# Alternating seven-product groups with usual ones, new bank places and a second bias-line buffer in an encoder kernel

## Chip, cores and metric

The kernel runs on one core of a Trainium2 chip. The metric is the device time of one execution in microseconds (us). Three runs of the kernel before gave 2324.68, 2325.39 and 2327.51 us, median 2325.39.

## The reference

A trunk of two layers over 256 positions of width 2048, all in float32. Layer 0 mixes tokens by grouped-query attention (mixer A), layer 1 by dilated window attention in three head groups with a shared relative bias (mixer B). Each is followed by a gated MLP of inner width 5632 with a convolution of width 3:

```python
def conv_ffn(h, w_up, conv_w, conv_b, w_down):
    u = h @ w_up
    c = u.shape[-1]
    pad = CONV_WIDTH // 2
    u = lax.conv_general_dilated(u, conv_w[:, None, :].astype(u.dtype), window_strides=(1,),
                                 padding=((pad, pad),), dimension_numbers=('NWC', 'WIO', 'NWC'),
                                 feature_group_count=c) + conv_b
    gate, val = jnp.split(u, 2, axis=-1)
    return (jax.nn.silu(gate) * val) @ w_down
...
        h = h + conv_ffn(rms_norm(h, ffn_norm[i]), w_up[i], conv_w[i], conv_b[i], w_down[i])
    return rms_norm(h, final_norm)
```

In mixer B the bias of a head is a table looked up by the distance of query and key; the kernel builds each head's line of values once and writes it to DRAM.

## The kernel before

**Products of float32 in three.** TensorE multiplies a reduced float format, so each operand is split into a high and a low part, and a product is taken as high x high, high x low and low x high. Weights come in tiles of 128x1024 (512 KB) by SyncE's queue (load_raw, L127; feed_T, L134) into six raw buffers; ScalarE makes the high part wh (split_raw, L119), VectorE the low part wl (L120). The parts go into a ring of three pairs of tiles, and of a fourth from the FFN's own pool (hl_ring, L608) during the down projection.

**The FFN** runs in two halves of 6 and 5 chunks of 512 inner columns (HALVES, L21). In a half, the up projection (feed_T: L143 for wh, L146 for wl) fills two banks ga and two banks va for each half chunk; up_post adds the two results (v, L446), scales (L448), convolves (L450 to L457) and applies silu; glu multiplies and splits into the tiles of activations ah and al (L468), or glu_forms into the seven combinations that a seven-product group needs. Then the down projection of this half's chunks: column blocks n = 0 and 1 together in project_pair, in the first half also 2 and 3; in the second half n = 2 and 3 come one by one by project (L164 to L166). add_residual (L386) or done (L559) adds the result to h.

**project_pair** treats a chunk either as a *usual* group: four units of 12 matmuls (128x512), which add straight into the four result banks C11, C21 (units 0, 1; block n0) and C12, C22 (units 2, 3; block n1), or as a *seven-product* group after Strassen and Winograd: seven units of 6 matmuls. Products 2, 3 and 4 go into C11, C12 and C21, the products 1, 5, 6 and 7 into banks of their own (M1, M5, M6, M7) that combine (L613 to L627: one copy on ScalarE and eight operations of 128x512 on VectorE) adds into h once the last product of the pair is out. Products 5, 7, 6 and 4 need the sum of two raw tiles (prepare, L240, on VectorE, put ahead in the order by high_priority). In both halves chunks 0 and 2 are seven-product groups (SKG). MIX sets the order: each seven-product group is interleaved with one usual group, in places two products next to each other; the usual groups that remain follow.

**Banks.** [...] new_acc (L187) alternates between b0, b1 and b2, b3; b4 to b7 are also turned over for small work by ps_tile. project_pair takes b4 to b7 for M1, M5, M6, M7 and b0 to b3, always in this order, for C11, C21, C12, C22 (L217). Which pair the up projection has just filled, and which the next new_acc takes, is in bank_at[0] and doesn't enter.

**Order.** A scheduler sets each engine's order at build time from the program's order and priorities; split_raw and the sums are 45 places ahead (AHEAD). Work that follows a stage (up_post, combine, the bias lines) is held as generators, of which step() runs one piece after each unit.

**Bias lines.** bias_lines (L870 to L891) is the side work of layer 0's first up projection: for each of six lines a matmul into a small bank (L885), a copy by VectorE into a tile ln (L888) and four DMAs by SyncE's queue to DRAM (scr0, scr1, L891). The tile has the tag "junk", of which there is one buffer. Lines 1 and 2 are 512 wide, the other four 256; each is written as four pieces, one per 32 of the 128 rows.

## Time and profile before

| | |
|---|---|
| three runs, median | 2325.39 us |
| the profiled execution | 2326.31 us |
| its span | 2324.5 us |
| mean granted TensorE clock | 0.996 |
| TensorE matmuls, busy | 11569, 2290.6 us (99% of the span) |
| VectorE busy | 1751.6 us (75%) |
| ScalarE busy | 1256.6 us (54%) |
| GpSimd busy | 168.8 us (7%) |
| weight loads of w_up, w_down (512 KB), issue to landing | 5.0 us, 5.3 us |

PE is TensorE, DVE VectorE, ACT ScalarE, POOL GpSimd, SP SyncE with its DMA queue (SPq). A row "L120 DVE ... wl<-raw,wh" is line 120 of the kernel, on VectorE, from tiles raw and wh to wl. A row of the timeline gives start, duration, and at its end in brackets the engine's idle time ahead and what ended it. A duration of a matmul is longer than its distance to the next, since they overlap; distances are taken from start to start. The clock is the share of full speed that the chip granted TensorE.

### The profile page before, as it was taken

How to read it: one execution, taken by the hardware profiler on the slowest of the kernel's cores; microseconds unless marked ns; L12 is line 12 of the kernel's file. 1: busy time of each engine (PE TensorE's matmuls, PEld its weight loads, DVE VectorE, ACT ScalarE, POOL GpSimd, SP SyncE). 2: the span in 40 equal slices, each digit the busy share in tenths (PEclk: the TensorE clock that was granted, in tenths of full speed). 3: DMA queues.
4: the chain of work that ended last, by engine and by line, in shares of the span. 5: the costliest groups of instructions: out<-in, count | busy, mean ns of one | idle time of the engine just before them, and what ended most of it. 6: DMA issues, size and time to landing. Idle time of an engine off the chain costs nothing.

```text
span 2324.5 us, 31224 instructions
## 1 busy us (share of the span) xinstructions
PE 2290.6 (99%) x11569; PEld 1935.9 (83%) x11569; DVE 1751.6 (75%) x2513; ACT 1256.6 (54%) x1816; POOL 168.8 (7%) x130
## 2 busy tenths in 40 slices
PE   9999999999999999999999999999999999999998
PEld 7788788888888888788888888878888878888876
DVE  6877876778867778968776876586777787777784
ACT  6565564555546556555554554355555544565553
POOL 2210010010000110000000000000101000001110
PEclk9999999999999999999999999999999999999999
DMA  8445665665666565566655565566566566666663
GB/s 296 155 138 161 191 193 174 211 198 181 207 198 187 188 189 172 200 213 197 197 173 174 180 190 164 178 188 196 185 195 188 168 209 208 182 190 186 195 208 127
DMA packets 260313, 437.54 MB, mean 188 GB/s; under 512 B 13904, under 2 KB 196944, under 8 KB 260160
## 3 DMA queue, kind: packets, MB, share of 16 engines
q1 hardware_dynamic: 258080, 429.84, 58.7%
q0 software_dynamic: 1648, 5.15, 0.8%
q8 instruction: 90, 1.47, 0.3%
q14 instruction: 63, 0.52, 0.1%
q10 hardware_dynamic: 432, 0.56, 0.1%
HBM read 429.20 MB, written 6.29 MB: 187 GB/s over the span
## 4 chain that ended last, share of the span: by engine, by line
PE 89%; DVE 5%; DMA 1%; issue 1%; ACT 1%; POOL 1%; SPq 0%; POOLq 0%; DVEq 0%; ACTq 0%
PE acc L143 27%; PE acc L146 14%; PE acc L165 11%; PE acc L166 11%; PE acc L164 11%; PE acc L271 4%; PE acc L273 4%; PE acc L276 4%; DVE wl L120 2%; DVE tT L332 1%; ACT wh L119 1%; DMA scr<-ln 1%; PE ps L303 1%; POOL cv L465 1%; PE ps L307 1%
## 5 line engine op out<-in xcount | busy, mean ns | idle before, releaser
L119 ACT ACTIVATE wh<-raw 128x1024 fp32r<-128x1024 f32 x828 | 872.7, 1058 | 779.3 <-PE acc L166 284.3
L120 DVE TENSOR_TENSOR wl<-raw,wh 128x1024 fp32r<-128x1024 f32 x828 | 1014.1, 1230 | 363.5 <-ACT wh L119 349.9
L143 PE MATMUL acc<-xh,wh 128*128 128x512 f32 x2816 | 709.6, 394 | 0.8 <-DVE h L386 0.8
L143 PEld LDWEIGHTS acc<-xh,wh 128*128 128x128 f32 x2816 | 508.3, 189 | 93.8 <-ACT wh L119 2.1
L146 PEld LDWEIGHTS acc<-xh,wl 128*128 128x128 f32 x2816 | 385.8, 191 | 36.1 <-DVE wl L120 8.4
L146 PE MATMUL acc<-xh,wl 128*128 128x256 f32 x2816 | 394.9, 283 | 7.6 <-DVE wl L120 7.6
L165 PE MATMUL acc<-wl,xh 128*128 128x512 f32 x768 | 300.3, 391 | 3.9 <-DVE wl L120 2.4
L164 PE MATMUL acc<-wh,xh 128*128 128x512 f32 x768 | 301.8, 394 | 0.0
L166 PE MATMUL acc<-wh,xh 128*128 128x512 f32 x768 | 299.6, 390 | 0.0
L271 PE MATMUL acc<-wh,ah 128*128 128x512 f32 x520 | 204.7, 394 | 3.6 <-DVE v L446 3.6
L273 PE MATMUL acc<-wh,al 128*128 128x512 f32 x520 | 204.3, 393 | 0.0
L164 PE MATMUL acc<-wh,ah 128*128 128x512 f32 x480 | 188.8, 393 | 2.4 <-DVE h L386 2.0
L165 PE MATMUL acc<-wl,ah 128*128 128x512 f32 x480 | 189.2, 394 | 2.0 <-DVE wl L120 1.8
L166 PE MATMUL acc<-wh,al 128*128 128x512 f32 x480 | 187.8, 392 | 0.0
L165 PEld LDWEIGHTS acc<-wl,xh 128*128 128x128 f32 x768 | 144.4, 188 | 34.2 <-DVE wl L120 4.9
L166 PEld LDWEIGHTS acc<-wh,xh 128*128 128x128 f32 x768 | 144.2, 188 | 30.0
L164 PEld LDWEIGHTS acc<-wh,xh 128*128 128x128 f32 x768 | 144.4, 188 | 28.1
L276 PE MATMUL acc<-wl,ah 128*128 128x512 f32 x520 | 148.0, 393 | 2.5 <-DVE wl L120 2.5
L271 PEld LDWEIGHTS acc<-wh,ah 128*128 128x128 f32 x520 | 97.6, 188 | 27.2 <-DVE v L446 5.4
L276 PEld LDWEIGHTS acc<-wl,ah 128*128 128x128 f32 x520 | 97.0, 188 | 27.1 <-DVE wl L120 5.9
L273 PEld LDWEIGHTS acc<-wh,al 128*128 128x128 f32 x520 | 97.6, 188 | 21.8
L165 PEld LDWEIGHTS acc<-wl,ah 128*128 128x128 f32 x480 | 90.6, 189 | 24.2 <-DVE wl L120 5.8
(175 smaller groups left out, 1843.7 us busy)
## 6 DMA issues: line engine op xcount, KB each, us to landing
raw<-in_w_up_dram SPq DMA_DIRECT2D x352, 512.0 KB, 5.0
raw<-in_w_down_dram SPq DMA_DIRECT2D x176, 512.0 KB, 5.3
raw<-in_w_b_dram SPq DMA_DIRECT2D x144, 512.0 KB, 4.3
raw<-in_w_bo_dram SPq DMA_DIRECT2D x48, 512.0 KB, 3.6
raw<-in_w_a_dram SPq DMA_DIRECT2D x40, 512.0 KB, 4.1
raw<-in_w_ao_dram SPq DMA_DIRECT2D x32, 512.0 KB, 3.5
raw<-in_w_a_dram SPq DMA_DIRECT2D x16, 256.0 KB, 5.5
h<-in_x_dram SPq DMA_DIRECT2D x4, 512.0 KB
```

Source lines behind the costliest of these rows:

```text
L119: nc.scalar.activation(wh, r, AF.Copy)
L120: nc.vector.tensor_tensor(wl, r, wh.bitcast(F32), ALU.subtract)
L143: nc.tensor.matmul(acc[j], wh[:, kt, j * P:(j + 1) * P], lhs[4 * kg + kt][2], start=first and i == 0 and kt == 0, stop=False)
L146: nc.tensor.matmul(acc[j][:, :NT], wl[:, kt, j * P:(j + 1) * P], lhs[4 * kg + kt][0], start=False, stop=end and kt == 3)
L164: nc.tensor.matmul(accs[m], xh, wh[:, j, :], start=st, stop=False)
L165: nc.tensor.matmul(accs[m], xh, wl[:, j, :], start=False, stop=False)
L166: nc.tensor.matmul(accs[m], xl, wh[:, j, :], start=False, stop=sp)
L271: nc.tensor.matmul(acc[k], xh, wh[:, j, :], start=k in fresh, stop=False)
L273: nc.tensor.matmul(acc[k], xl, wh[:, j, :], start=False, stop=False)
L276: nc.tensor.matmul(acc[k], xh, wl[:, j, :], start=False, stop=last[k] == i and j == 1)
L303: nc.tensor.matmul(o, lh[ls], rh[rs], start=start, stop=stop)
L307: nc.tensor.matmul(o, ll[ls], rh[rs], start=False, stop=stop)
```

## The change

1. Bias lines get a tag of their own with two buffers.
2. SKG is given per half: chunks 0 and 2 in the first, chunk 0 alone in the second.
3. The order of units: first a usual unit, then product, usual, product, usual, one by one, products in the order 1, 2, 5, 3, 7, 6, 4; the rest of the usual units follow. In the first half (14 products, 16 usual units) the last product is unit 28 of 30, in the second (7 and 16) unit 14 of 23.
4. C11 and C21 take the two banks that the last new_acc did not take (2 - b, 3 - b), which the next new_acc takes too; C12 and C22 take the other two.
5. What is left of combine is run before the second block's sums end the pair (finished); in the second half also before block n0 is added.
6. The three tiles u of the convolution are 528 floats wide in place of 516, rb 32 in place of 24.

```diff
-SKG = (0, 2)
-MIX = (("P", 1), ("c", 0), ("P", 2), ("P", 5), ("c", 1), ("P", 3), ("P", 7), ("c", 2), ("P", 6), ("P", 4), ("c", 3))
+SKG = ((0, 2), (0,))
+ORDER = (1, 2, 5, 3, 7, 6, 4)
...
-        acc = {k: bank((4, 5, 6, 7, 0, 1, 2, 3)[i], "acc") for i, k in enumerate(place)}
+        b = bank_at[0]
+        acc = {k: bank((4, 5, 6, 7, 2 - b, 3 - b, b, b + 1)[i], "acc") for i, k in enumerate(place)}
...
-            us = [fp.tile([P, 2, 258], F32, name=nm("u")) for _ in range(3)]
+            us = [fp.tile([P, 528], F32, name=nm("u"))[:, :516].rearrange("p (j c) -> p j c", j=2) for _ in range(3)]
...
-                    if p - p0 in SKG:
+                    if p - p0 in SKG[hf]:
...
-                ckg = [k for k in range(np_) if k not in SKG]
-                units = []
-                for k in SKG:
-                    c = ckg.pop(0)
-                    units += [("c", c, u[1]) if u[0] == "c" else ("P", k, u[1]) for u in MIX]
-                units += [("c", c, i) for c in ckg for i in range(4)]
+                cs = [("c", k, i) for k in range(np_) if k not in SKG[hf] for i in range(4)]
+                ps = [("P", k, p) for k in SKG[hf] for p in ORDER]
+                per = max((len(cs) - 4) // len(ps), 1)
+                units = [cs.pop(0)]
+                for u in ps:
+                    units += [u] + [cs.pop(0) for _ in range(per)]
+                units += cs
+                late_at = next(i for i, u in enumerate(units) if u[1] == np_ - 1)
...
+                    combined.append((n0, n1))
+
+                def finished(n0, n1):
+                    while (n0, n1) not in combined:
+                        step()
+
+                def first_half(a, n0, n1):
+                    if hf == 1:
+                        finished(n0, n1)
+                    done((a["C11"], a["C21"]), n0)
...
-                    acc = project_pair(wd, n0, n1, slots, forms, units, len(units) - 4 if late else None,
+                    acc = project_pair(wd, n0, n1, slots, forms, units, late_at if late else None,
                                        lambda a: start(combine(a, n0, n1)),
-                                       lambda a: done((a["C11"], a["C21"]), n0))
+                                       lambda a: first_half(a, n0, n1))
                     done((acc["C12"], acc["C22"]), n1)
-
+                    finished(n0, n1)
+
+                combined = []
...
-            rb = lp.tile([P, 24], F32, name="rb")
+            rb = lp.tile([P, 32], F32, name="rb")[:, :24]
...
-                ln = lp.tile([P, 512], F32, tag="junk", name=nm("ln"))
+                ln = lp.tile([P, 512], F32, tag="ln", name=nm("ln"), bufs=2)
```

**Loads at the first pair's entry.** SyncE's loads of w_down in layer 0's first half, from the first one, before. 1018 is block 11 of the first seven-product group, 1022 the usual unit 0, 1025 block 21, 1026 block 12, 1034 block 22.

```order
L127 DMA raw_1018_5322<-in_w_down_dram 128x1024
L127 DMA raw_1022_5342<-in_w_down_dram 128x1024
L127 DMA raw_1025_5365<-in_w_down_dram 128x1024
L127 DMA raw_1026_5367<-in_w_down_dram 128x1024
L127 DMA raw_1031_5394<-in_w_down_dram 128x1024
L127 DMA raw_1034_5412<-in_w_down_dram 128x1024
L127 DMA raw_1039_5435<-in_w_down_dram 128x1024
```

The same place afterwards: 1018 is usual unit 0, 1022 block 11, 1028 block 21, 1032 block 12, 1040 block 22.

```order
L127 DMA raw_1018_5322<-in_w_down_dram 128x1024
L127 DMA raw_1022_5348<-in_w_down_dram 128x1024
L127 DMA raw_1025_5365<-in_w_down_dram 128x1024
L127 DMA raw_1037_5430<-in_w_down_dram 128x1024
L127 DMA raw_1028_5387<-in_w_down_dram 128x1024
L127 DMA raw_1031_5399<-in_w_down_dram 128x1024
L127 DMA raw_1032_5401<-in_w_down_dram 128x1024
L127 DMA raw_1040_5448<-in_w_down_dram 128x1024
```

The usual unit now comes first, and block 12, which the fifth product's sum needs, has moved from the fourth load to the seventh.

**VectorE at the same entry**, before: sums of raw tiles (L240), splits (L120) and up_post's work on the last two accumulators (L446 to L457).

```order
L446 TENSOR_TENSOR v_1001_5237<-acc_981_5105,v_1001_5237 128x256
L240 TENSOR_TENSOR raw_1018_5322<-raw_1018_5322,raw_1026_5367 128x1024
L120 TENSOR_TENSOR wl_1009_5295<-raw_1005_5272,wh_1008_5294 128x1024
L448 TENSOR_TENSOR u_535_2604<-v_1001_5237,rbc_537_2609 128x4x128
L120 TENSOR_TENSOR wl_1024_5345<-raw_1022_5342,wh_1023_5344 128x1024
L455 SCALAR_TENSOR_TENSOR cg_978_5102<-u_535_2604,cw_533_2602,cg_978_5102 128x256 x2
L457 SCALAR_TENSOR_TENSOR cg_978_5102<-u_535_2604,cw_533_2602,cg_978_5102 128x256 x2
L240 TENSOR_TENSOR raw_1026_5367<-raw_1026_5367,raw_1034_5412 128x1024
L120 TENSOR_TENSOR wl_1028_5371<-raw_1025_5365,wh_1027_5370 128x1024
L120 TENSOR_TENSOR wl_1030_5385<-raw_1018_5322,wh_1029_5384 128x1024
L446 TENSOR_TENSOR v_1021_5334<-acc_982_5106,v_1021_5334 128x256
L446 TENSOR_TENSOR v_1021_5334<-acc_983_5107,v_1021_5334 128x256
```

Afterwards (all lines are one higher there):

```order
L447 TENSOR_TENSOR v_1001_5237<-acc_981_5105,v_1001_5237 128x256
L449 TENSOR_TENSOR u_535_2604<-v_1001_5237,rbc_537_2609 128x4x128
L120 TENSOR_TENSOR wl_1009_5295<-raw_1005_5272,wh_1008_5294 128x1024
L456 SCALAR_TENSOR_TENSOR cg_978_5102<-u_535_2604,cw_533_2602,cg_978_5102 128x256 x2
L458 SCALAR_TENSOR_TENSOR cg_978_5102<-u_535_2604,cw_533_2602,cg_978_5102 128x256 x2
L120 TENSOR_TENSOR wl_1024_5351<-raw_1022_5348,wh_1023_5350 128x1024
L241 TENSOR_TENSOR raw_1022_5348<-raw_1022_5348,raw_1032_5401 128x1024
L120 TENSOR_TENSOR wl_1027_5368<-raw_1025_5365,wh_1026_5367 128x1024
L120 TENSOR_TENSOR wl_1030_5390<-raw_1028_5387,wh_1029_5389 128x1024
L447 TENSOR_TENSOR v_1021_5340<-acc_982_5106,v_1021_5340 128x256
L447 TENSOR_TENSOR v_1021_5340<-acc_983_5107,v_1021_5340 128x256
L241 TENSOR_TENSOR raw_1032_5401<-raw_1032_5401,raw_1040_5448 128x1024
```

Both sums of the first products stood ahead of the last reads of the up projection's accumulators (acc_982, acc_983); now one does, and it waits for the seventh load.

**VectorE at the end of the first half** (before; acc_1109 and acc_1110 are C11 and C21, acc_1111 and acc_1112 C12 and C22, h_82 the residual):

```order
L386 TENSOR_TENSOR h_82<-acc_1109_5810,h_82 128x512
L120 TENSOR_TENSOR wl_1224_6308<-raw_1221_6303,wh_1223_6307 128x1024
L386 TENSOR_TENSOR h_82<-acc_1110_5811,h_82 128x512
L120 TENSOR_TENSOR wl_1226_6328<-raw_1222_6305,wh_1225_6327 128x1024
L386 TENSOR_TENSOR h_82<-acc_1111_5812,h_82 128x512
L120 TENSOR_TENSOR wl_1230_6352<-raw_1227_6347,wh_1229_6351 128x1024
L386 TENSOR_TENSOR h_82<-acc_1112_5813,h_82 128x512
```

Afterwards (L387 is add_residual, L621 to L630 combine):

```order
L387 TENSOR_TENSOR h_82<-acc_1109_5810,h_82 128x512
L624 TENSOR_TENSOR cu_1191_6230<-acc_1108_5809,cu_1191_6230 128x512
L625 TENSOR_TENSOR h_82<-h_82,cu_1192_6231 128x512
L387 TENSOR_TENSOR h_82<-acc_1110_5811,h_82 128x512
L120 TENSOR_TENSOR wl_1224_6308<-raw_1221_6303,wh_1223_6307 128x1024
L627 TENSOR_TENSOR h_82<-h_82,cu_1191_6230 128x512
L629 TENSOR_TENSOR cu_1191_6230<-acc_1106_5807,cu_1191_6230 128x512
L120 TENSOR_TENSOR wl_1226_6328<-raw_1222_6305,wh_1225_6327 128x1024
L387 TENSOR_TENSOR h_82<-acc_1111_5812,h_82 128x512
L120 TENSOR_TENSOR wl_1230_6352<-raw_1227_6347,wh_1229_6351 128x1024
L387 TENSOR_TENSOR h_82<-acc_1112_5813,h_82 128x512
L630 TENSOR_TENSOR h_82<-h_82,cu_1191_6230 128x512
```

C11 and C21 are read ahead of the first split of the next up projection (wl_1224) rather than around it, and it is their banks that the up projection writes first; combine now stands here too.

## Prediction

> **What bounds the kernel now.** I read the page first, then TensorE's waits, then the timeline around each wait, and last the granted clock in stretches. The page's row of engines:
>
> ```profile
> PE 2290.6 (99%) x11569; PEld 1935.9 (83%) x11569; DVE 1751.6 (75%) x2513; ACT 1256.6 (54%) x1816; POOL 168.8 (7%) x130
> ```
>
> TensorE is busy 99% of the span, so time goes only if matmuls go, if they run faster, or if one of its waits goes. Its waits, largest first ("longest" is the last number):
>
> ```profile
> PE acc L146 <- DVE wl L120: 7.6, 2, 4.3
> PE acc L271 <- DVE v L446: 3.6, 4, 2.6
> PE acc L276 <- DVE wl L120: 2.5, 4, 0.6
> PE acc L164 <- DVE h L386: 2.0, 1, 2.0
> PE acc L143 <- DVE h L386: 0.8, 2, 0.4
> PE acc L164 <- DVE h L559: 0.4, 1, 0.4
> ```
>
> These six rows are 16.9 us, and each stands at a place that the diff touches: two in the first up projection (bias lines), four at the entries of the down projection's pair part, four in its first mixed group, four at its exits. A busy TensorE need not be a fast one, so I looked at the clock behind these waits (columns: busy time of five engines, clock, DMA share, GB/s):
>
> ```profile
> 394.00:399.00 5.00, 1.73 (x8) 1.14 (x7) 3.24 (x6) 1.49 (x3) 0.00 (x0) 0.94 0.25 70
> 399.00:402.00 3.00, 3.00 (x12) 2.71 (x12) 2.33 (x5) 0.55 (x1) 1.64 (x1) 0.53 0.23 81
> 428.00:431.00 3.00, 2.99 (x11) 2.80 (x12) 2.67 (x5) 0.90 (x1) 1.29 (x1) 0.50 0.65 192
> ```
>
> After the two waits of the first row the clock drops to about half for some 3 us (D shows a third place). That time is busy time in every other view, and it goes with the wait.
>
> **A. The second bias-line buffer.** TensorE around the first stall, and at the end of the second:
>
> ```profile
> 390.60 2.00 PE L143 MATMUL acc<-xh,wh 128*128 128x512 f32 x8
> 392.44 1.11 PE L146 MATMUL acc<-xh,wl 128*128 128x256 f32 x8
> 393.39 2.00 PE L143 MATMUL acc<-xh,wh 128*128 128x512 f32 x8
> 398.66 2.07 PE L146 MATMUL acc<-xh,wl 128*128 128x256 f32 x8 [3.27 <-DVE wl L120]
> ...
> 402.98 1.11 PE L146 MATMUL acc<-xh,wl 128*128 128x256 f32 x8
> ```
> ```profile
> 421.68 2.00 PE L143 MATMUL acc<-xh,wh 128*128 128x512 f32 x8
> 428.01 2.08 PE L146 MATMUL acc<-xh,wl 128*128 128x256 f32 x8 [4.33 <-DVE wl L120]
> ...
> 432.95 0.28 PE L146 MATMUL acc<-xh,wl 128*128 128x256 f32 x1
> ```
>
> An undisturbed tile (eight long, eight short matmuls) takes 393.39 - 390.60 = 2.79 us; its long half 392.44 - 390.60 = 1.84, so one long matmul starts every 0.23. So 393.39 + 1.84 = 395.23 was due and 398.66 came: 3.43. From there to 402.98, short half plus long half, are 4.32 where 2.79 are usual: 1.53. The second place: 428.01 - 421.68 - 1.84 = 4.49, and 432.95 - 428.01 - 2.79 = 2.15. Together 11.6 us. Why VectorE was late:
>
> ```profile
> 395.73 0.69 DVE L888 COPY ln<-ps 128x512 f32<-128x512 f32 x1 [9.63 <-DMA scr<-ln]
> 425.01 0.42 DVE L888 COPY ln<-ps 128x256 f32<-128x256 f32 x1 [8.87 <-DMA scr<-ln]
> ```
>
> Line 2's copy (L888) goes into the one buffer that line 1's write to DRAM still reads, and the weight split (L120) stands behind the copy in VectorE's order. With two buffers line 2 waits for nothing and line 4 waits for line 2's write, not line 3's. What is late next? The writes do not get shorter, and SyncE's queue holds weight loads behind them:
>
> ```profile
> 381.98 13.45 DMA scr<-ln
> 416.67 8.06 DMA scr<-ln
> 379.99 3.06 SPq L891 DMA_DIRECT2D scr<-ln  x4
> 412.38 1.06 ACT L119 ACTIVATE wh<-raw 128x1024 fp32r<-128x1024 f32 x1 [1.00 <-DMA raw<-in_w_up_dram]
> 413.82 1.06 ACT L119 ACTIVATE wh<-raw 128x1024 fp32r<-128x1024 f32 x1 [0.38 <-DMA raw<-in_w_up_dram]
> ```
>
> Write 1 runs from 379.99 to 381.98 + 13.45 = 395.43, 15.4 us; the first load issued behind write 2 is the one that ScalarE gets at 412.38, the sixth tile after that of 393.39. Unstalled it is due at 393.39 + 6 x 2.79 = 410.1, and in SBUF by 409.0 (ScalarE's split is 1.06). If write 2, now queued right behind write 1, ends 8.06 us after it (what line 3's last piece took), the load is there at 395.4 + 8.1 + 1.4 = 404.9 (1.4 is the step between the two ScalarE rows): no stall. If it takes another 15.4, it lands at 412.2: 3.2 of stall. I take 1.5, nearer to the middle since part of the 15.4 is waiting behind loads. **A = -10.1** (-11.6 to -8.4, and -6.3 if the clock drops again).
>
> **B. Entries of the pair part.** The worst entry:
>
> ```profile
> 2205.42 0.39 PE L271 MATMUL acc<-wh,ah 128*128 128x512 f32 x1
> 2208.41 0.50 PE L271 MATMUL acc<-wh,ah 128*128 128x512 f32 x1 [2.60 <-DVE v L446]
> ```
> Start to start this costs 2.99 - 0.23 = 2.76, 0.16 more than the wait shown. The waits view has 3.6 for all four, so the other three cost 1.0 + 3 x 0.16 = 1.5: 4.3 in all. The first usual unit writes the banks that the last up projection has just filled and v (L446) has yet to read. Afterwards it writes the other two, read out a whole tile pair ago; the late ones come up with usual unit 2, after two usual and two product units of 12 and 6 matmuls, 36 x 0.23 = 8.3 us in, beyond the 2.76. **B = -4.3** (to -1.5 if VectorE's order there hurts instead).
>
> **C. Inside the first mixed group.**
>
> ```profile
> 572.93 0.40 PE L273 MATMUL acc<-wh,al 128*128 128x512 f32 x1
> 573.94 0.74 PE L276 MATMUL acc<-wl,ah 128*128 128x512 f32 x2 [0.61 <-DVE wl L120]
> ```
>
> 1.01 - 0.23 = 0.78, at each of four entries: two product units stand next to each other (3 and 7) and VectorE cannot give two sums, two splits and the activation work in 2.7 us. VectorE is full there:
>
> ```profile
> 555.00:606.00 51.00, 50.17 (x218) 40.16 (x217) 45.19 (x49) 28.10 (x33) 3.24 (x1) 1.00 0.65 208
> ```
>
> Alternating one by one spreads the same sums over longer PE time, and second halves lose four of eight sums per layer (L240, 1.22 us each). **C = -3.1** (-4.6 with the smaller gaps beside them, +2 if the sums move badly).
>
> **D. Exits.**
>
> ```profile
> 961.10 1.10 PE L276 MATMUL acc<-wl,ah 128*128 128x512 f32 x4
> 964.22 0.48 PE L164 MATMUL acc<-wh,ah 128*128 128x512 f32 x1 [2.02 <-DVE h L386]
> ...
> 965.00 0.60 PE L164 MATMUL acc<-wh,ah 128*128 128x512 f32 x1
> ...
> 968.38 0.43 PE L166 MATMUL acc<-wh,al 128*128 128x512 f32 x1
> ```
>
> Stall: 964.22 - 961.10 - 4 x 0.23 = 2.20. Slow clock: eight matmuls from 965.00 to 968.38, 3.38 where 1.84 are usual: 1.54. The other three exits wait 0.4 each by the waits view, near 0.58 start to start: 1.7. Now the next accumulators take the banks of the first block, which were added to h two usual units (24 matmuls, 5.5 us) earlier. **D = -5.5** (to -2).
>
> [...]
>
> **E. Tile places.** A usual unit whose weights lie in the FFN's own pool, and one whose weights do not:
>
> ```profile
> 638.04 0.40 PE L271 MATMUL acc<-wh,ah 128*128 128x512 f32 x1
> ...
> 639.90 1.07 PE L276 MATMUL acc<-wl,ah 128*128 128x512 f32 x4
> ...
> 642.19 0.39 PE L271 MATMUL acc<-wh,ah 128*128 128x512 f32 x1
> ...
> 644.00 1.07 PE L276 MATMUL acc<-wl,ah 128*128 128x512 f32 x4
> ```
>
> Eight matmuls take 1.86 and 1.81: 6 ns each. By the pools' layout this goes with the two operands lying differently against 128 bytes; padding moves that pool by 32 bytes, from one kind of mismatch to another. What surely goes: second halves need 24 activation tiles, all in the other pool, where 28 left four in this one, for 288 matmuls: 288 x 6 ns = 1.7. **E = -1.7** (0 to -4.9, if all such matmuls, 815 by the same layout, are cured).
>
> **F. Matmuls.** A seven-product group has 42, a usual one 48; per layer one group in the second half becomes usual for one column pair: +6, two layers +12, at 0.23: **F = +2.8**.
>
> **G. New waits by the alternation: 0.** Loads:
>
> ```profile
> raw<-in_w_down_dram SPq DMA_DIRECT2D x176, 512.0 KB, 5.3
> ```
>
> Six raw buffers; a usual unit's buffer inside the mixed stretch is used again after two usual and two product units, 8.3 us later (before, after 42 to 48 matmuls, 9.6 to 11.0). Less the split, 1.06 + 1.23, 6.0 are left against 5.3 from issue to landing. Tight but covered; ends 0 and +6.
>
> **Sum**: -10.1 - 4.3 - 3.1 - 5.5 - 1.7 + 2.8 = -21.9, made against the profiled execution's 2326.3 us (0.9 above the median of the three, 2325.4): 2304.4, or 2303.5 on the median. I say 2304.
>
> **Rivals.**
> 1. *The bias writes hold up the loads.* If write 2 takes a whole further 15.4 us, the load is 3.2 late, the clock falls again (some 1.8), and A gains 5 rather than 10: 2309. For: in 394 to 399 the DMA share is 0.25, a quarter of the engines do the writes. Against: line 3's last piece needed only 8.06, though with half the bytes. Chance 0.17.
> 2. *VectorE waits for the sum's load.* The fifth product's sum now needs the seventh load in SyncE's order, and stands ahead of splits on VectorE.
>
> ```profile
> 2204.52 1.22 DVE L240 TENSOR_TENSOR raw<-raw,raw 128x1024 f32<-128x1024 f32 x1 [2.49 <-DMA raw<-in_w_down_dram]
> ```
> If four entries each pay such a 2.5, +10: 2314. Against: this sum is due with the sixth unit, 48 matmuls or 11 us in. Chance 0.10.
> 3. *The other side: the raw buffers' chain.* Ten product groups with three tight links each; when a load takes L, each link costs L - 6.0, less a lead of about 3.2 per group (9.6 to 11.0 spacing less 2.3 and 5.3) from the units ahead. 30 (L - 6.0) - 32 equals the gain of 21.9 at L = 7.8; from there the change loses. At 8.3 it is 37 - 21.9 = +15: 2341. Against: 5.3 median, at a DMA share of 0.65. Chance 0.11, of which L from 7.6 to 8.0 (within 0.2%) holds 0.06 and more 0.05.
>
> **How the numbers follow.** Forecast 0.62, rivals 0.17, 0.10, 0.11. The low end is every term at its best: 2326.3 - 11.6 - 4.3 - 4.6 - 5.5 - 4.9 + 2.8 = 2298; the high end takes in rivals 1 and 2 with a little more: 2317. A measurement of this kernel can tell about 0.2% (4.7 us) from no change. Faster 0.88, same 0.07, slower 0.05.
>
> **What would show it.** A: no L888 copy with a DMA wait on VectorE, TensorE's L146 row gone from the waits or under 2 us, clock 1.00 around 400 and 430; the first up projection some 10 us shorter. B: no wait for v at pair entries. C: no wait in the L276 row. D: no wait for h at exits, clock 1.00 at 965. E: units at 1.81 per eight in second halves. F: 11,581 matmuls. G and rival 3: w_down loads above 7 us and ScalarE waiting on raw inside the mixed stretches. The forecast is wrong if the waits for weights inside the pair parts come to more than a few us.

## The result, and the profile after

Four runs gave 2300.06 to 2301.36 us, median 2300.95, against 2326.01 of the kernel before: a ratio of 0.9892 with a 95% interval of 0.9874 to 0.9909, 25.1 us less. The forecast was 2304 (2298 to 2317). The profiled execution took 2300.93 us, 25.4 less than the one before, where the sum of the prediction had 21.9.

The page's engine row and TensorE's waits, all of them, in the changed kernel (lines behind 217 stand one or more higher than before):

```profile
PE 2281.6 (99%) x11581; PEld 1935.0 (84%) x11581; DVE 1732.5 (75%) x2483; ACT 1248.6 (54%) x1802; POOL 168.5 (7%) x130
```
```profile
PE acc L165 <- DVE wl L120: 3.9, 9, 0.9
PE ps L375 <- DVE warm L372: 1.5, 1, 1.5
PE acc L165 <- DVE wl L176: 1.4, 1, 1.4
PE ps L308 <- DVE qTl L290: 0.8, 1, 0.8
PE acc L143 <- ACT wh L119: 0.8, 1, 0.8
```

All six rows that the prediction built on are gone; what is left belongs to mixers A and B and to the program's start, but for the last row, which is new. The busy time of TensorE fell by 9 us although it has twelve matmuls more. The slow clock, which counted as busy, is 5.2 of this by the prediction's three figures (1.53, 2.15, 1.54); most of the rest lies in the four pair parts. Here an entry is the place where TensorE passes from an up projection to the pair part, an exit the place where it leaves the pair part, and a stall is time in which it starts no matmul though the last one's share (0.23 us, or 0.12 for a short one) is over. At the stages' ends, before (first column: from, to; then length, busy times of the five engines, clock, DMA share, GB/s), the first up projection and the four pair parts:

```profile
269.90:555.00 285.10, 277.50 (x1563) 242.69 (x1563) 207.09 (x316) 159.04 (x239) 27.14 (x21) 0.98 0.63 197
555.00:684.30 129.30, 128.07 (x555) 103.20 (x553) 104.50 (x107) 65.18 (x68) 3.24 (x1) 1.00 0.62 197
...
907.80:964.20 56.40, 53.46 (x230) 42.43 (x229) 51.94 (x62) 30.97 (x39) 3.25 (x1) 1.00 0.61 205
...
1850.50:1980.00 129.50, 128.01 (x554) 103.17 (x552) 104.67 (x108) 65.19 (x68) 3.25 (x1) 1.00 0.61 196
...
2203.60:2260.60 57.00, 53.38 (x231) 42.41 (x229) 49.73 (x55) 30.95 (x39) 7.54 (x3) 1.00 0.60 199
```

and after:

```profile
269.10:543.60 274.50, 273.74 (x1562) 239.84 (x1561) 206.89 (x315) 158.78 (x239) 27.27 (x21) 1.00 0.64 205
543.60:670.20 126.60, 126.60 (x554) 103.67 (x553) 103.75 (x106) 64.84 (x68) 3.25 (x1) 1.00 0.62 200
...
893.70:947.30 53.60, 53.60 (x237) 43.96 (x236) 43.08 (x51) 28.18 (x35) 2.12 (x1) 1.00 0.63 206
...
1831.40:1958.40 127.00, 127.00 (x555) 103.69 (x554) 103.73 (x106) 65.02 (x68) 3.25 (x1) 1.00 0.61 199
...
2181.80:2235.50 53.70, 53.70 (x236) 43.88 (x235) 43.17 (x48) 28.07 (x35) 6.32 (x3) 1.00 0.63 206
```

In the four pair parts busy time now equals length: TensorE does not stand still there at all, with six matmuls more in each of the two short ones. From the exact starts of the stages, which the windows above round:

| stretch | before | after | difference | terms of the prediction |
|---|---|---|---|---|
| program's start to the first up projection | 269.9 | 269.1 | -0.8 | none |
| first up projection | 285.0 | 274.5 | -10.5 | A: -10.1 |
| four pair parts | 372.3 | 360.8 | -11.5 | B -4.3, C -3.1, stalls of D -3.9, F +2.8, part of E |
| 964.2 to the second layer's up projection | 616.5 | 614.4 | -2.1 | clock of D -1.5, part of E |
| the other up projections | 716.8 | 716.7 | -0.1 | none |
| last stage (n = 2, 3) | 55.4 | 55.0 | -0.4 | part of E |

The remainder of A that was forecast stands there too. TensorE and ScalarE around it, after:

```profile
409.24 1.11 PE L146 MATMUL acc<-xh,wl 128*128 128x256 f32 x8
411.11 2.11 PE L143 MATMUL acc<-xh,wh 128*128 128x512 f32 x8 [0.76 <-ACT wh L119]
```
```profile
410.00 1.06 ACT L119 ACTIVATE wh<-raw 128x1024 fp32r<-128x1024 f32 x1 [7.99 <-DMA raw<-in_w_up_dram]
411.42 1.06 ACT L119 ACTIVATE wh<-raw 128x1024 fp32r<-128x1024 f32 x1 [0.37 <-DMA raw<-in_w_up_dram]
```

The first load behind line 2's write reaches ScalarE at 410.00. It was due by 409.0, and the stall is 0.92 from start to start (411.11 - 409.24 - 0.95, the short half of an undisturbed tile). The clock stays at 1.00 (408 to 412). Line 2's copy now stands where the program has it, with no wait:

```profile
384.85 0.68 DVE L903 COPY ln<-ps 128x512 f32<-128x512 f32 x1
```

### The profile page after: what moved, and what is told of

Its sections match the earlier page's. It is cut to its first block, busy times and chain, and to the rows that moved or that the text cites. A ratio compares the mean times of both kernels' runs of the same rounds, so it can differ in the third digit from the quotient of the medians.

```text
span 2299.2 us, 31196 instructions
## 1 busy us (share of the span) xinstructions
PE 2281.6 (99%) x11581; PEld 1935.0 (84%) x11581; DVE 1732.5 (75%) x2483; ACT 1248.6 (54%) x1802; POOL 168.5 (7%) x130
## 4 chain that ended last, share of the span: by engine, by line
PE 93%; DVE 3%; DMA 1%; issue 1%; POOL 1%; ACT 0%; SPq 0%; POOLq 0%; DVEq 0%; ACTq 0%
PE acc L143 28%; PE acc L146 14%; PE acc L165 11%; PE acc L166 11%; PE acc L164 11%; PE acc L272 5%; PE acc L274 5%; PE acc L277 5%; DVE wl L120 1%; DVE tT L333 1%; PE ps L304 1%; DMA raw<-in_w_up_dram 1%; PE ps L308 1%; PE ps L307 1%; PE ps L306 0%
## 5 line engine op out<-in xcount | busy, mean ns | idle before, releaser
L120 DVE TENSOR_TENSOR wl<-raw,wh 128x1024 fp32r<-128x1024 f32 x822 | 1007.7, 1231 | 369.5 <-ACT wh L119 356.8
L466 POOL TENSOR_TENSOR cv<-cg,cv 128x512 f32<-128x512 f32 x32 | 73.2, 2288 | 651.6 <-DVE cv L458 591.2
L277 PEld LDWEIGHTS acc<-wl,ah 128*128 128x128 f32 x524 | 98.4, 188 | 21.8
```

The lines of the kernel that those rows point to most:

```text
L120: nc.vector.tensor_tensor(wl, r, wh.bitcast(F32), ALU.subtract)
L277: nc.tensor.matmul(acc[k], xh, wl[:, j, :], start=False, stop=last[k] == i and j == 1)
L466: nc.gpsimd.tensor_tensor(cv, cg, cv, ALU.mult)
```

## Experiments

Medians are set against 2325.9 to 2326.4 us of the kernel before, run beside each experiment, and against 2300.95 of the changed kernel from its own set of runs. Stage lengths are from each run's profile, which is one execution.

**1. The second bias-line buffer alone.**

```diff
-                ln = lp.tile([P, 512], F32, tag="junk", name=nm("ln"))
+                ln = lp.tile([P, 512], F32, tag="ln", name=nm("ln"), bufs=2)
```

> The kernel before with only the second bias-line buffer (a tag of its own, two buffers). Theory: the two stalls of 3.43 and 4.49 us in the first up projection go and with them the two stretches at half clock behind them (1.53 and 2.15), less a rest of about 0.9 at the first load behind line 2's write, as the changed kernel's trace has it (one gap of 0.92 at 410): the first up projection, 285.0 us before, is 274 to 275 long, the kernel -10.5 (ratio 0.9955), and every other stage stays within 0.5 us. Rival 1, the slow clock is not caused by the stalls: only 7.9 - 0.9 = 7 us go and the clock around 400 and 430 is still low. Rival 2, the writes' queue takes it back: with the pair part's timing as before, a new wait for a weight tile of 3 us or more behind line 2's write, -5 to -7.

2316.30 us, ratio 0.9959 (0.9944 to 0.9974), -9.8. Stretches of its profile, the first up projection and the place behind the layer's second-half exit:

```profile
269.70:543.40 273.70, 273.70 (x1562) 239.83 (x1561) 207.16 (x316) 158.84 (x239) 27.28 (x21) 1.00 0.65 205
952.80:956.80 4.00, 3.97 (x18) 3.31 (x19) 3.90 (x8) 2.37 (x5) 0.00 (x0) 1.00 0.37 120
```

The stage lost 11.3 us, nearly all of the 11.6 of stalls and slow clock, here without the 0.92. Rivals 1 and 2 are out. But the second row is a surprise: the same wait of 2.0 us for h at the exit (2.19 start to start, before 2.20) is still there, and the clock behind it is 1.00. In the kernel before it was 0.63:

```profile
964.00:968.00 4.00, 3.78 (x11) 3.02 (x12) 3.91 (x8) 1.45 (x4) 0.00 (x0) 0.63 0.41 123
```

The reverse stands at the last entry, where this profile has a slow clock and the kernel before has none, although no edit reaches it:

```profile
2196.00:2200.00 4.00, 3.65 (x9) 2.88 (x10) 2.36 (x4) 0.00 (x0) 0.00 (x0) 0.50 0.26 76
```

This pair part is 60.3 us long against 57.0. So "every other stage within 0.5 us" failed, at both places by the slow clock (experiment 12).

**2. The bank places alone.**

```diff
-        acc = {k: bank((4, 5, 6, 7, 0, 1, 2, 3)[i], "acc") for i, k in enumerate(place)}
+        b = bank_at[0]
+        acc = {k: bank((4, 5, 6, 7, 2 - b, 3 - b, b, b + 1)[i], "acc") for i, k in enumerate(place)}
```

> The kernel before with only the new places of C11, C21, C12 and C22. Theory: the waits for v at the four entries (2.76, 0.39, 0.50, 0.64 us start to start) and the waits for h at the four exits (2.20 and three of 0.58) go, and the slow clock behind the 2.20 (1.54), 9.7 us in all; the old order keeps its waits for wl in the mixed group (0.78 four times). So -9.7 (ratio 0.9958), provided that the old order touches the other two banks late enough: its third usual unit is unit 7, after 2 usual and 5 product units, 12.4 us in, so nothing new at entries. Rival: the exits don't come from the banks but from VectorE being behind with combine, which starts at the last product either way; then the wait for h at 962 only moves or shrinks, and the gain is about 4.3, that of the entries.

2314.58 us, ratio 0.9951 (0.9936 to 0.9966), -11.5. No wait for v or for h is left at any entry or exit, so the exits do come from the banks and not from combine. TensorE's waits at the pair parts are those for wl, beside one of 0.3 us for wh:

```profile
PE acc L277 <- DVE wl L120: 2.0, 5, 0.6
```

It gained 1.8 more than was expected: the gaps in the mixed groups of the first halves fell from 0.78 to 0.59 and 0.38 too, but in the last pair part two of 0.78 stand where there was one.

**3. The order alone** (one group in second halves, alternation, forced combine; the changed kernel with old banks, one bias-line buffer, no padding).

```diff
-        b = bank_at[0]
-        acc = {k: bank((4, 5, 6, 7, 2 - b, 3 - b, b, b + 1)[i], "acc") for i, k in enumerate(place)}
+        acc = {k: bank((4, 5, 6, 7, 0, 1, 2, 3)[i], "acc") for i, k in enumerate(place)}
...
-            us = [fp.tile([P, 528], F32, name=nm("u"))[:, :516].rearrange("p (j c) -> p j c", j=2) for _ in range(3)]
+            us = [fp.tile([P, 2, 258], F32, name=nm("u")) for _ in range(3)]
...
-            rb = lp.tile([P, 32], F32, name="rb")[:, :24]
+            rb = lp.tile([P, 24], F32, name="rb")
...
-                ln = lp.tile([P, 512], F32, tag="ln", name=nm("ln"), bufs=2)
+                ln = lp.tile([P, 512], F32, tag="junk", name=nm("ln"))
```

> The kernel before with only the new order of units: one group instead of two in second halves, alternation one by one, and the forced rest of combine; banks in their old places, bias lines in one buffer, no padding. Theory: the mixed groups' waits go (0.78 four times, 1.15 with the small gaps beside them: -3.1 to -4.6), twelve more matmuls come (+2.8), 288 matmuls lose their odd tile places (up to -1.7); but the first unit is now a usual one that writes the banks the last up projection filled, so the entries' waits get longer than with the product first, whose own bank was free: v is read some 3 us into the pair, so each entry waits 2 to 3 us (before 0.4 to 2.8), +3 to +8; exits as before or longer, since combine and the sums come together. In all 0 to +8 (ratio 1.000 to 1.0035), with A's stalls still there. Rival: order and banks are independent, the entries' waits stay at 4.3 in all, and the sum is -1 to -3.

2325.86 us, ratio 1.000 (0.999 to 1.0009). At the pair parts there remain:

```profile
PE acc L271 <- DVE v L446: 4.6, 4, 3.2
...
PE acc L164 <- DVE h L386: 2.2, 1, 2.2
...
PE acc L143 <- DVE h L386: 0.8, 2, 0.4
```

The waits for wl in the mixed groups are gone, twelve matmuls came, and the entries wait 4.6 instead of 3.6. The expected lengthening to 2 or 3 us came at one entry (3.33 start to start) and not at the other three (0.64 or less); the time fits the lower end of the theory, and the rival, a gain of 1 to 3, fits no better.

**4. The padding alone.**

```diff
-            us = [fp.tile([P, 2, 258], F32, name=nm("u")) for _ in range(3)]
+            us = [fp.tile([P, 528], F32, name=nm("u"))[:, :516].rearrange("p (j c) -> p j c", j=2) for _ in range(3)]
...
-            rb = lp.tile([P, 24], F32, name="rb")
+            rb = lp.tile([P, 32], F32, name="rb")[:, :24]
```

> The kernel before with only the padded tiles (u to 528 floats, rb to 32), which moves the FFN's own pool from places of 32 to places of 0 in 128 bytes; every wait stays. Theory: the mismatch with the other operand stays, of another kind; a matmul with one operand in that pool goes from 233 to about 231 ns (in the changed kernel's trace 231.5 against 228 for those without), so 815 x 2 ns = -1.6 us at most (ratio 0.9993 to 1.000). Rival: padding brings these to the speed of the others, -4 (ratio 0.998). The run is also a second profile of the old stalls: if the half clock hangs on them, it stands again behind the stalls at 395, 423 and 962 and not behind the 2.76 at 2205; if it was chance of one execution, at other places.

2324.94 us, ratio 0.9998 (0.9989 to 1.0007): no difference that ten runs show. The rival's -4 is out; the theory's -1.6 lies inside the interval and can't be told from nothing. Its profile has the old stalls again, and the clock behind the exit of layer 0 and behind the last entry reads:

```profile
964.30:968.30 4.00, 4.00 (x18) 3.32 (x19) 3.90 (x8) 2.39 (x5) 0.00 (x0) 1.00 0.38 130
2206.20:2209.60 3.40, 3.40 (x10) 2.67 (x9) 1.66 (x2) 0.13 (x1) 0.00 (x0) 0.50 0.38 111
```

Behind a stall of 2.25 the clock stayed, behind one of 2.28 it fell; in the kernel before it was the other way round at these two places. So neither the place nor the length decides.

**5. Both groups in second halves, alternating as long as usual units last.**

```diff
-SKG = ((0, 2), (0,))
+SKG = ((0, 2), (0, 2))
...
-                    units += [u] + [cs.pop(0) for _ in range(per)]
+                    units += [u] + [cs.pop(0) for _ in range(min(per, max(len(cs) - 1, 0)))]
```

> The changed kernel, but with seven-product groups 0 and 2 in second halves too (12 matmuls fewer over the two layers), alternating as long as usual units last; the last four products follow one another, with one usual unit behind. Theory: those products stand side by side with sums and splits on VectorE (per product 1.37 us of TensorE against 1.2 of sum and 1.2 of split), so TensorE waits for wl there, some 1 us per product after the first, and for h at the exit because combine starts one unit before the end: second-half pairs 53.6 us now would be 55 to 58, the kernel +3 to +9. Rival: VectorE is far enough ahead after the alternating stretch, no new wait, and the twelve matmuls are pure gain, -2.8 (ratio 0.9988 to the changed kernel).

2310.89 us, 9.9 slower than the changed kernel, a little beyond the +9 that was expected at most. New waits:

```profile
PE acc L164 <- DVE h L387: 2.2, 1, 2.2
PE acc L164 <- DVE h L560: 2.2, 1, 2.2
...
PE acc L272 <- ACT wh L119: 1.4, 1, 1.4
```

Both exits wait 2.2 for h, one with the slow clock behind it (0.50 from 953.1 to 956.5); the last entry waits 1.4 for wh, and small gaps stand inside the two pair parts. On VectorE, in layer 0, TensorE's stall ends with the second of these sums (L387), in front of which combine (L621 to L629) runs:

```profile
945.87 0.68 DVE L621 TENSOR_TENSOR cu<-acc,cu 128x512 f32<-128x512 f32 x1
...
951.13 0.68 DVE L387 TENSOR_TENSOR h<-acc,h 128x512 f32<-128x512 f32 x1
951.74 0.68 DVE L629 TENSOR_TENSOR cu<-acc,cu 128x512 f32<-128x512 f32 x1
952.33 0.68 DVE L387 TENSOR_TENSOR h<-acc,h 128x512 f32<-128x512 f32 x1
```

The exit of the theory is right; the waits for wl between the products, which made up most of the expected loss inside the pair parts, did not come (53.0 and 55.5 long, 53.6 and 53.7 in the changed kernel). The rival is out.

**6. The second half's products two by two, four usual units behind the last.**

```diff
-SKG = ((0, 2), (0,))
+SKG = ((0, 2), (0, 2))
...
-                units = [cs.pop(0)]
-                for u in ps:
-                    units += [u] + [cs.pop(0) for _ in range(per)]
+                units = []
+                for g in (1, 2, 2, 2, 2, 2, 2, 1) if hf else (1,) * 14:
+                    units += [cs.pop(0)] + [ps.pop(0) for _ in range(g)]
                 units += cs
```

> The changed kernel with two seven-product groups in second halves, as in two_groups, but the products two by two between usual units (1, 2, 2, 2, 2, 2, 2, 1), so that four usual units stay behind the last product. Theory: two_groups lost at the exit, where h came 2.2 us late because combine began one unit before the end; with four usual units (11 us) behind the last product, combine (5.4 us on VectorE), two sums and four splits just fit, the exits wait for nothing, and the 12 matmuls fewer are a gain: second-half pairs 52.4 to 53.5 us (53.6 and 53.7 in the changed kernel), the kernel -2.4 to 0 against it. Rival: the density of products is what VectorE cannot take; waits for wl and for sums inside the stretch come to 1 to 3 us per pair and the kernel is 1 to 5 us slower than the changed one.

2298.54 us (2298.06 to 2299.48), ratio 0.9879 (0.9865 to 0.9894) to the kernel before, 2.4 under the changed kernel, whose runs (2300.06 to 2301.36) lie wholly above. The two were not run beside each other, and the intervals of their ratios overlap; the stage lengths show the gain more plainly. Its second-half pair parts:

```profile
893.10:945.40 52.30, 52.30 (x230) 42.84 (x229) 48.69 (x55) 31.03 (x38) 1.28 (x1) 1.00 0.62 206
2180.10:2232.50 52.40, 52.40 (x229) 42.78 (x229) 48.56 (x53) 31.09 (x38) 5.30 (x3) 1.00 0.63 208
```

No wait, and 1.3 us less in each: six matmuls at 0.23 are 1.4. VectorE is busy 48.7 of 52.3 us and still keeps up. So what made one group per second half look right was mainly how the units stood at the end (this order also spreads the products more evenly, and the two were not tried apart), and term F could have been saved.

**7. Bias lines and banks together, the old order.** The two diffs of 1 and 2.

> The kernel before with the second bias-line buffer and the new bank places together, the old order kept. Theory: the parts add up: -9.8 and -11.5 from the two runs alone make -21.3, 2304.7 us, and what the new order does on top of the banks (and the padding) is the rest to the changed kernel's 2301, some -3 to -4, though it runs 12 matmuls (2.8 us) more. Rival: they overlap (the second layer's last entry shifts with the time of its load), the sum is -18 or less; or the order brings nothing once the banks are right, and this kernel is within 1 us of the changed one.

2304.97 us (2303.57 to 2306.13), ratio 0.9904 (0.9888 to 0.9921); -21.3 makes 2304.7. The parts add up. The order, with the padding, brings 4.0 on top, although alone it brings nothing: with the old banks its gain in the mixed groups went into twelve more matmuls (2.8), longer waits at the entries (1.0) and, in that profile, the slow clock behind the longest of them (0.57 from 2206 to 2210). What is left without it:

```profile
PE acc L277 <- DVE wl L120: 3.1, 6, 0.6
PE acc L272 <- ACT wh L119: 1.6, 1, 1.6
```

With the smaller gaps beside them these come to 6.8 us start to start; less the 2.8 for matmuls that leaves 4.0.

**8. All operands at one place in 128 bytes.**

```diff
         with tc.tile_pool(name=nm("fpool"), bufs=1) as fp:
+            fp.tile([P, 16], F32, name=nm("gap"))
             junk = junk_of(fp)
```

> The changed kernel with an unused tile of 64 bytes at the start of the FFN's pool, so that all operands of its matmuls lie at 64 in 128 bytes. Theory: a matmul is slower when its two operands lie differently against 128 bytes (231.5 ns against 228 in the changed kernel's trace), so the some 650 matmuls concerned gain 3 ns each, -2 us (ratio 0.9991), and the spread of spacings in the pair parts vanishes: 227 to 229 everywhere. Rival: the spacing hangs on the pool's distance or the bank, not on the place in 128 bytes; nothing changes, the time is the changed kernel's within 0.5 us.

2302.00 us (2299.88 to 2302.32): not faster. The matmuls of the pair parts, by form, in the changed kernel and then here (busy time, mean ns of one):

```profile
L272 PE MATMUL acc<-wh,ah 128*128 128x512 f32 x524 | 205.7, 393 | 0.0
...
L277 PE MATMUL acc<-wl,ah 128*128 128x512 f32 x524 | 146.9, 391 | 0.0
```
```profile
L272 PE MATMUL acc<-wh,ah 128*128 128x512 f32 x524 | 205.5, 392 | 0.0
...
L277 PE MATMUL acc<-wl,ah 128*128 128x512 f32 x524 | 146.8, 391 | 0.0
```

These are durations; the distances from start to start say more. The first pair part is 126.0 long against 126.6, and it is 126.0 again in experiments 10 and 11, which have the same unused tile, so a small part of the theory may be true. The other three pair parts are the same to 0.2. In the second layer the mean distance is still 229.8 and 229.4 ns (230.0 and 229.1 in the changed kernel), where 227 to 229 was expected everywhere. So the theory behind term E, that a matmul is slower when its operands lie differently in 128 bytes, does not explain the spacing: with all at the same place most of the differences remain. The times show no gain.

**9. Bias lines on GpSimd's queue.**

```diff
-                    nc.sync.dma_start(dst[:, 32 * i:32 * i + 32, :], ln[:, :w])
+                    nc.gpsimd.dma_start(dst[:, 32 * i:32 * i + 32, :], ln[:, :w])
```

> The changed kernel with the bias lines written by GpSimd's queue and not by SyncE's. Theory: the rest of 0.92 us at 410 is a weight tile whose load stands behind line 2's write in SyncE's ring; in a ring of its own the write shares the engines instead, the load lands earlier and the gap goes: -0.9 us (ratio 0.9996), the first up projection 273.6 long instead of 274.5. Rival: the write's transfer itself is what takes the engines, whatever its queue; the gap stays or grows to 1 to 2 us.

2300.90 us (2300.08 to 2302.14). The first up projection is 273.2 long and without the gap. But shift64 (273.8), two_spread (273.8) and ln_only have none either, with SyncE's queue. So the 0.92 belongs to some executions. By its length the stage does gain a little from the queue: 273.2 in all three profiles with GpSimd's (experiments 9 to 11), 273.7 to 273.9 in the five without the gap on SyncE's. The times do not show it.

**10. 8 and 9 together.**

> The changed kernel with the unused 64-byte tile of shift64 and the bias lines on GpSimd's queue together. Theory: the pair parts of shift64 were 0.6 us shorter in all, and the gap of 0.92 behind the line's write is missing with the other queue: -0.6 to -1.5 against the changed kernel, 2299.5 to 2300.3, at the edge of what five rounds can tell. Rival: both were differences of single executions (the first 6 to 8 us of the program alone vary by 2 us between profiles), and the time is that of the changed kernel within 0.5 us.

2300.22 us (2299.20 to 2301.28), 0.7 under the changed kernel, within the spread of both. Not decided.

**11. 6, 8 and 9 together.**

> two_spread with the unused 64-byte tile and the bias lines on GpSimd's queue. Theory: two_spread is faster than the changed kernel because 12 matmuls (2.76 us) are gone and nothing waits in their place, so another build of it, with small things moved in the pool and the queues, is again at 2297.5 to 2299, its second-half pairs again 52.2 to 52.5 us long; the other two edits bring 0 to -0.7. Rival: two_spread's 2298.5 was a lucky order at the edge of what VectorE can do; with the small shifts a wait of 1 to 2 us comes up in one of the second halves and the time is 2299.5 to 2301.

2296.91 us (2296.47 to 2297.20), ratio 0.9873 (0.9856 to 0.9889): the fastest version, 4.0 under the changed kernel. The first up projection and the two second-half pair parts:

```profile
269.20:542.40 273.20, 273.20 (x1562) 239.76 (x1561) 207.76 (x315) 159.48 (x239) 44.11 (x45) 1.00 0.68 206
891.90:944.00 52.10, 52.10 (x231) 42.86 (x230) 48.65 (x55) 31.11 (x38) 1.29 (x1) 1.00 0.63 207
2178.50:2230.90 52.40, 52.40 (x231) 42.91 (x231) 48.35 (x53) 31.38 (x38) 5.51 (x3) 1.00 0.63 209
```

Two_spread's gain is there again. The other two edits seem to bring 1.6 beside it and 0.7 without it. Against experiment 6 the profile is 1.3 shorter: 0.55 in the first up projection (the queue), 0.57 in the first pair part (the tile's place), 0.5 in the other three pair parts, less 0.3 at the end of the program. In experiment 10 the same 0.3 is lost at the end, and 0.4 each at the program's start and in the last pair part; what these come from isn't settled.

**12. Stalls of known lengths.** In split_raw the subtraction is issued n times more, at chunks 2, 4, 7 and 9.

```diff
+        n, probe[0] = probe[0], 0
...
+            for _ in range(n):
+                nc.vector.tensor_tensor(wl, r, wh.bitcast(F32), ALU.subtract)
             nc.vector.tensor_tensor(wl, r, wh.bitcast(F32), ALU.subtract)
...
+                            if hh == 1:
+                                probe[0] = ({2: 3, 4: 4, 7: 5, 9: 6}, {2: 6, 4: 5, 7: 4, 9: 3})[l].get(p, 0)
```

> The changed kernel with the subtraction of one weight split repeated 3, 4, 5 or 6 times more (1.23 us each) at eight places of the up projections, chunks 2, 4, 7 and 9 of both layers, so that TensorE stalls there by known and different lengths; the output does not change. Theory: the drop of the clock behind a stall depends on the stall's length and on the moment: always behind more than about 3.4 us, sometimes between 2 and 3.4, never below 2; each drop costs 1.5 to 2.3 us beyond the stall. Rival: any stall that ends in a full queue of matmuls is followed by the drop, or none below 3.4 is and the drop behind the 2.20 of the kernel before had another cause.

2327.88 us in one run, with stalls of 1.3 to 4.2 us. Two of them, the first with a short wait and a drop behind it, the second with a long one and none:

```profile
407.53 0.59 PE L907 MATMUL ps<-oh,lh 128*128 128x256 f32 x2
409.95 3.42 PE L148 MATMUL acc<-xh,wh 128*128 128x512 f32 x8 [1.83 <-ACT wh L122]
```
```profile
746.62 1.22 PE L151 MATMUL acc<-xh,wl 128*128 128x256 f32 x8 [3.02 <-DVE wl L125]
```
```profile
410.40:413.80 3.40, 3.40 (x11) 2.75 (x10) 3.23 (x4) 2.97 (x6) 0.00 (x0) 0.50 0.89 274
743.00:748.00 5.00, 1.98 (x13) 1.51 (x12) 4.66 (x7) 1.26 (x2) 0.00 (x0) 1.00 0.65 212
```

Length alone does not decide, which rules out both rivals; and the stall of 3.62 in the table below, without a drop, rules out the theory's "always behind more than about 3.4" (in the kernel before, a drop follows the stalls of 3.43 and 4.49). All drops behind these stalls last 3.413 or 6.827 us in the trace's record of the clock, and begin a whole number of 3.413 us after the record's first entry: in the kernel before at 398.40, 425.71 and 965.01, which is 115, 123 and 281 times 3.4133 behind the entry at 5.87. So I divided each run's time into windows of 3.413 us from that entry, and took for every stall of more than 1.2 us past the program's start, in all profiles, the largest part of one window that it covers. Ten of them:

| stall, us | run, place | largest share of one window | clock drop |
|---|---|---|---|
| 2.19 | ln_only, 950.7 | 0.47 | no |
| 2.25 | pad_only, 962.0 | 0.49 | no |
| 3.18 | clock_probe, 743.4 | 0.50 | no |
| 2.75 | before, 2205.7 | 0.53 | no |
| 3.62 | banks_only, 394.4 | 0.53 | no |
| 2.09 | clock_probe, 407.9 | 0.61 | yes |
| 2.19 | before, 962.0 | 0.64 | yes |
| 2.28 | pad_only, 2203.6 | 0.67 | yes |
| 2.35 | two_groups, 950.7 | 0.69 | yes |
| 3.33 | order_only, 2202.7 | 0.84 | yes |

Of 29 stalls all 15 with 0.61 or more were followed by a drop, and of the 14 with 0.53 or less none but one (ln_only, 2193.5), which shares its window with another stall of 0.8 us, together 0.60. With the idle time of each window added up like this, the line lies at just about 0.60: the largest sum without a drop is also 0.60 (pad_only, the window from 421.0). The rule was read off these profiles; no run was made to test it. It does not cover how long a drop lasts: two of the four of 6.827 us went on through a window with 0.24 or less of idle time.

## Why the prediction was right, and where it was off

- **What bounds it.** Right: the six rows of waits and the slow clock behind them were most of what could go, and they went. Two smaller things went too: short gaps beside the waits and a few ns between matmuls.
- **A** (-10.1): the stage lost 10.5, with the edit alone 11.3. The load behind line 2's write was placed at 404.9 to 412.2 and came at 410.0; 0.92 of stall where 1.5 was taken, and it does not come in every execution. Rival 1 did not happen. Its slow clock, too, was that of one execution: behind the same two stalls stand three windows of 3.413 us in the profile of the kernel before, but three, two and one in order_only, pad_only and banks_only. That may be one reason why experiment 1 gained 9.8 in its runs and not 11.3. (The four DMAs of a line each write the whole tile, 256 KB at a width of 512, to other rows of the target, not a quarter of it: a write is 1 MB.)
- **B** (-4.3) **and D's stalls** (-3.9): all eight waits are gone, by the banks alone (experiment 2).
- **D's slow clock** (-1.5): mis-sized. In the profile of the kernel before, the stall covers 0.64 of one window of 3.413 us and the drop follows; of three other profiles with this stall none has a drop behind it (clock 1.00 in ln_only, order_only and pad_only; in ln_only it covers 0.47 of a window, in pad_only 0.49). It was in the profiled execution, so it is in the difference of profiles, but by these four only a part of it is a gain of the kernel. An idle share of 0.61 of a window was the lowest with a drop behind the stall (experiment 12).
- **C** (-3.1): the term that was too small. With the small gaps beside each wait it is 1.15 at each of four places, 4.6, which the prediction gave as an end of the range; all of it went with the order alone (experiment 3). Over the pair parts, stalls and gaps start to start were 13.2 us before and 0.1 after, where B, C and D's stalls had 11.3. Experiment 7 says the same from the other side: without the new order the pair parts still wait, and it is 4.0 slower.
- **E** (-1.7): the size came, the reason did not hold, so this is luck in part. Start to start and without gaps, matmuls of the second halves stand 1.0 to 1.9 ns closer (230.0 and 230.1 ns before, 229.0 and 229.1 after in the pair parts; 229.7 and 229.8, then 227.8 and 228.6 in the blocks n = 2, 3), 1.2 us in all, and those of the first halves' pair parts 0.8 and 0.3 ns closer, another 0.6. But the step "this goes with the two operands lying differently against 128 bytes" failed (experiment 8), and padding alone shows nothing in the times (experiment 4). What sets these few ns remains open.
- **F** (+2.8): right, and shown by its reversal: 1.3 us less for six matmuls fewer (experiment 6).
- **G and rivals 2 and 3** (0): right for TensorE, for the reason given. VectorE does wait for the sums' loads far more than before, in this row before and after:

```profile
DVE raw L240 <- DMA raw<-in_w_down_dram: 11.4, 10, 2.5
```
```profile
DVE raw L241 <- DMA raw<-in_w_down_dram: 29.7, 15, 4.8
```

Up to 4.8 us, yet nothing that TensorE needs in that time stands behind it; the sum is due 11 us in. Rival 2's mechanism came, its price did not. Loads of w_down land faster, not slower (4.4 us, 5.3 before), so rival 3 was far off:

```profile
raw<-in_w_down_dram SPq DMA_DIRECT2D x176, 512.0 KB, 4.4
```

- **The sum** was 3.5 short of the profiles' difference: 1.9 in the gaps of the pair parts, 1.5 of them in C, 0.8 ahead of the first up projection, where no edit reaches and the profiles differ by 2 us among themselves, 0.4 in A, and a few tenths elsewhere. That the measured time is 3 us from the forecast and no more owes something to luck as well, since the slow clock of A and D is not the same in every execution.

## What to carry to other kernels

Look at the granted clock behind every stall of the bounding engine: a stall of 3.43 us cost 4.96 in this kernel (1.53 of it slow clock), and the share of busy time, 99% before and after, hid the difference. Where accumulators rotate, let a stage that mixes two kinds of work first write the banks that were read out longest ago and be done early with those that the next stage takes; here this was the largest single edit by the medians (-11.5, against -9.8 for the buffer). An order can look bad mainly for its end: the same denser units cost 9.9 us with one usual unit behind the last product and gained 2.4, evenly spread, with four.

## What was not expected of the hardware

In these profiles the clock drops keep to windows of 3.413 us, counted from the first entry of the record: a stall of 2.09 us brought one on and one of 3.62, split evenly over two windows, did not. A window of drop cost about 1.5 us (1.53 and 1.54 in the kernel before). The first window of the record begins 4.4 to 7.6 us after the first instruction, differently in each profile (5.87 in the kernel before, 4.97 in the changed one), so the windows lie differently against the stalls. That the same kernel therefore has different drops from run to run is the author's estimate. The times leave room for it: the kernel before ranged from 2323.05 to 2328.14 us over 19 runs, the changed kernel from 2300.06 to 2301.36 over four. The recorded clocks agree: of the 19 runs the three with a mean granted clock of 0.998 took 2323.05 to 2324.66 us, the four with 0.995 2326.48 to 2328.14. That nothing else adds to the spread is not shown.
